# A two-layer transformer trunk on one core: the last Down units by accumulator, ScalarE's order fixed at gate/up, smaller and later loads

## The chip, the cores and the metric

The kernel runs on one core of one Trainium2 chip, in one launch. A core has five engines that run their own instruction streams side by side: TensorE (PE, the matmuls; PEld are its weight loads), VectorE (DVE), ScalarE (ACT), GpSimd (POOL) and SyncE (SP, which here only issues DMAs). An engine takes its instructions strictly in the order of its program; an instruction that waits for another engine holds up all that stand behind it. The metric is device time in microseconds (us): the median of several runs of the whole kernel.

## The reference, cut to what matters

The kernel computes two layers of an encoder trunk over one sequence of 1024 tokens with 1024 features, all in fp32. `mod` is a matrix product of a condition vector with large weights (adaLN). There are two layers, the hidden width F is 2816, and `ya`, `yb`, `yc` are three attentions over parts of `proj`; `yc` normalises its q and k, times `gq_ax` and `gk_ax`, and turns them by rotary tables.

```python
cond = jax.nn.silu(c)
for l in range(DEPTH):
    mod = cond @ w_mod[l] + b_mod[l]
    sh_a, sc_a, gt_a, sh_f, sc_f, gt_f = [m[:, None, :] for m in split_cols(mod, (D,) * 6)]
    h = rms_norm(x, g_attn[l]) * (1 + sc_a) + sh_a
    proj = h @ w_in[l]
...
    y = jnp.concatenate([rms_norm(ya, ga), rms_norm(yb, gb), rms_norm(yc, gc)], axis=-1)
    x = x + gt_a * (y @ w_o[l])

    h = rms_norm(x, g_ffn[l]) * (1 + sc_f) + sh_f
    gate, up = split_cols(h @ w_gu[l], (F, F))
    x = x + gt_f * ((jax.nn.silu(gate) * up) @ w_down[l])
return rms_norm(x, g_final)
```

## The kernel before

**Arithmetic.** An fp32 product is made of three TensorE matmuls: each operand is split into a high part (`...h`, `hi`, a rounded CAST on ScalarE) and the remainder (`...l`, `lo`, a subtraction on VectorE or GpSimd), and high x high, low x high and high x low are added in a PSUM bank (`mm3`). The feed-forward products go by a Strassen-like scheme with 7 products of quarter size in place of 8; the operands of some products are sums of blocks. `PRODUCTS` lists the seven of a quad of gate/up with the operand of the activations and one of three PSUM banks: `(1,"11",a) (2,"21",b) (6,"t2",a) (5,"t1",c) (7,"t3",a) (3,"22",c) (4,"t4",a)`. Products on the same bank follow each other, and each stands on the sum already in it; before product 7 adds onto bank a, ScalarE must have copied product 6 out of it (`COPY sg<-ps_w`), and so on.

**Stages of a layer.** Norm and input projections (`ps_c`, `ps_ab`, `ps_v`); attention (the middle of the layer); output projection (`ps_o`); gate/up (`ps_w`); Down (`ps_d`). Gate/up has 22 quads q, of 7 products with 12 matmuls each. Of the first 7 quads (`EARLY`) products 1 and 2 are made first, since their activations (`ht`... from blocks `11`, `21`) are ready soonest; after them come products 6, 5, 7, 3, 4 of quads 0 to 6, then quads 7 to 21 whole. The operands `t3`, `22` and `t4` of the activations (`ht3h/ht3l`, `h22h/h22l`, `ht4h/ht4l`) are made from the blocks `xb` of x by `t3_part` and `t4_part`, row block by row block, between these two loops. They overwrite `xb`, whose memory (tags x0 to x3) is then used for the raw weights of odd quads: `wr` (a DMA of 512 KB into x2 and one into x3) and their sums `ws`. A class `Ahead` makes the parts of the weights (`wpt`, hi by ScalarE, lo by VectorE or GpSimd) up to 8 products ahead of their use: `ahead.get()` first fills to 8, then hands out one.

Down has 7 products in the order 1, 2, 6, 7, 4, 5, 3, of 11 units each, 77 units u in all. A unit has four banks (`acc_a` or `acc_b`, one for each 128 output features) with 3 matmuls each, 12 in all; at the end of most products `residual` adds a bank to the block `xb` of x. Beside the units a generator `beside` takes a step for each: the squares of the finished half of x, its 1/rms (`rstd`), and in the last layer the turned, scaled output of that half (`out_turn`: four PE transposes into `ps_f`; `out_scale`: times 1/rms and g_final, `gf`, then a DMA out). In layer 0 it is the norm of the next layer instead.

Beside gate/up of layer 0, from quad 7 on, `mod_stream` makes adaLN products that are needed later on VectorE (`acc`), splits them (`acch`, `accl`), and `mod_flush` sums them over partitions by two matmuls a piece (`ps_mod`). Each `yield` hands control back to the loop of products.

**What sets the order.** All instructions are issued through a helper, `issue` in the class `Engine`, so that every row of the profile has its line, L49, and one goes by the names of tiles. A scheduler orders the instructions of each engine by its own estimates, unless the engine is pinned: `pin([act], True)` makes each further ScalarE instruction depend on the one issued before it, so that ScalarE has them in the order in which the code issues them. Before, SP is pinned in gate/up and Down, and ScalarE and VectorE in some places, not where gate/up begins.

Of the kernel before, what the change touches and what calls it, by code (L numbers as in the profile page):

```python
# [19 lines left out]
P = 128  # L20
D = 1024
S = 1024
KC = D // P
H = 512
FF = 2816
NF = FF // P
NB = NF // 2
# [53 lines left out]
def bc(ap, shape):  # L81
    return ap.to_broadcast(shape)
# [3 lines left out]
def trunk(ctx: ExitStack, tc, A, C, out):  # L86
# [5 lines left out]
    def pin(engines, on):  # L92
        for e in engines:
            e.pinned = on
# [260 lines left out]
    def mod_stream(psp, shared, until):  # L355


        pl, tag, bufs, width = shared
        acc = None
        while todo and todo[0] < until:  # L360
            l, g = todo[0]
            first = going["step"]
            if first == 0:
                going["acc"] = cp.tile([P, 1024], F32, name="acc", tag="acc")
            acc = going["acc"]
            halves = [(k, c0) for k in range(first, KC) for c0 in range(0, 1024, width)]
            loads = {}

            def load(i):
                k, c0 = halves[i]  # L370
                st = loads[i] = pl.tile([P, width], F32, name="wmt", tag=tag, bufs=bufs)
                g0 = g * 1024 + c0
                sp.dma_start(st, A["w_mod"][l, k * P : (k + 1) * P, g0 : g0 + width])

            if halves:
                load(0)
                yield
            for i, (k, c0) in enumerate(halves):
                if i + 1 < len(halves):
                    load(i + 1)  # L380
                mod_add(k, acc[:, c0 : c0 + width], loads.pop(i))
                yield
            going["step"] = KC
            mod_parts(slice(0, width), shared)
            while going["step"]:
                yield
                yield
                mod_flush(psp)
            yield

# [145 lines left out]
    cc_cm, ccp = open_pool("cc", side="right")  # L536
# [4 lines left out]
    csts = []  # L541
# [4 lines left out]

    def gains_load(pl, l):
        g8 = pl.tile([P, 8, 64], F32, name="g8")
        sp.dma_start(g8[:, 0:6, :], bc(A["gq_ax"][l][None, None, :], [P, 6, 64]))
        sp.dma_start(g8[:, 6:8, :], bc(A["gk_ax"][l][None, None, :], [P, 2, 64]))  # L550
        pool.tensor_scalar(
            out=g8[:, 0:6, :], in0=g8[:, 0:6, :], scalar1=0.125, scalar2=None, op0=ALU.mult
        )
        for _ in range(4):
            rope_load(pl)
        return g8
# [260 lines left out]
    for l in range(2):  # L817
# [1100 lines left out]
        for q in range(EARLY):  # L1918
            for i in range(2):
                a = [w[:, 4 * i : 4 * i + 4] for w in early[q]]  # L1920
                gu_product(q, PRODUCTS[i], a)
            if q + 4 < EARLY:
                early.append(first_cols((q + 4) % 2 * FF + (q + 4) // 2 * 2 * P))
            elif raw0 is None:
                raw0 = gu_raw(0)
            if q == 0:
                next(norm)
            if q == 1:
                rows = next(norm)
            if 1 <= q < 5:  # L1930
                bs.append(t2_part(q - 1, rows))
            if q == 1:
                t3_part(0, *bs[0])
                t4_part(0, *bs[0])
            if q == EARLY - 2:
                ahead.fill(5)
        for part in (t3_part, t4_part):
            for q in range(1, 4):
                part(q, *bs[q])
        pin([sp], True)  # L1940
        for q in range(NF):
            if q % 2 == 0:
                gu_start(q // 2)
            if q < EARLY:
                up = q % 2
                e = sg[q // 2][0][:, 0:H]
                if up:
                    pool.tensor_tensor(out=e, in0=e, in1=quads[q]["11"], op=ALU.mult)
            for i, p in enumerate(PRODUCTS[2 if q < EARLY else 0 :]):
                gu_product(q, p, ahead.get())  # L1950
                if i == 1 and q < EARLY and not up:
                    act.activation(e, quads[q]["11"], AF.Silu)
                ahead.fill()
                g_step()
                if q >= EARLY:
                    next(mods_due, None)
# [7 lines left out]
        def out_turn(half, j, nh):  # L1964

            t0 = half * H + j * P
            ps = psl.tile([P, 4, P], F32, name="ps_f", tag="mm")
            for i in range(4):
                pe.transpose(ps[:, i, :], xt[:, nh * 4 + i, t0 : t0 + P], ident)
            return half, j, nh, ps.rearrange("p a b -> p (a b)")  # L1970
# [122 lines left out]
        def square_add(ssq, n, half):  # L2093
            sq = square(n, half, "sq", 2)
            dve.tensor_tensor(out=ssq, in0=ssq, in1=sq, op=ALU.add)
# [20 lines left out]
        def odd_squares():  # L2116
            odd.append(square(1, 1, "ssqo", 1))
            yield
            for n in (3, 5, 7):
                square_add(odd[0], n, 1)  # L2120
                yield

        beside = iter(())
        for u in range(NU):
            i, t = divmod(u, NB)
            num, _, bank = DOWN[i]
            for what in due.get(u, ()):
                what()
            ahead.fill(4)
            if u % 2 == 0 and (u + 6) // 2 <= (NU - 1) // 2:  # L2130
                b_load((u + 6) // 2)
            for _ in range(3 if steps else 0):
                g_step()
            if u == 5:
                xt = blocks(xp)
            if t == 0 and num == 2:
                acc_b = [psl.tile([P, 512], F32, name="ps_d", tag="mm") for _ in range(4)]
            banks = acc_a if bank == "a" else acc_b
            a, b = ahead.have.pop(0)
            for j in range(4):  # L2140
                js = slice(j * P, (j + 1) * P)
                mm3(
                    banks[j], a[:, 0, js], a[:, 1, js], b[:, 0], b[:, 1],
                    num in (1, 2, 5) and t == 0, t == NB - 1, skip_group_check=True,
                )
            next(beside, None)
            if u >= NU - 2 and not last_layer:
                if u == NU - 2:
                    wC = []
                wC.append(split_w(w_in_src(1, C_COLS, len(wC)), 2, eng=dve))  # L2150
            if t < NB - 1:
                continue
            m, half = {
                1: (0, 0), 2: (0, 0), 6: (0, 1), 7: (1, 1), 4: (1, 0), 5: (1, 1), 3: (0, 1),
            }[num]
            for j in range(4):
                residual(banks[j], 2 * j + m, slice(half * H, half * H + H), 40)
            if num == 4:
                close(w2_cm)
                close(w1_cm)  # L2160
                if last_layer:
                    fn_cm, fnp = open_pool("fin", side="right")
                    gf = fnp.tile([P, D], F32, name="gf")
                    sp.dma_start(gf, bc(A["g_final"][None, :], [P, D]))
                else:
                    h_cm, hp = open_pool("h", side="right")
                    hh = hp.tile([P, KC, S], F32R, name="hh")
                    hl = hp.tile([P, KC, S], F32R, name="hl")
                    cc_cm, ccp = open_pool("cc", side="right")
                    csts.clear()  # L2170
                    g8 = gains_load(ccp, 1)
                    spill(0)
                beside = chain(early_half(), odd_squares())
        for _ in beside:
            pass
        pin([sp], False)
        pin((act, dve), not last_layer)
        for n in range(0, KC, 2):
            square_add(odd[0], n, 1)
        if last_layer:  # L2180
            blocks_ = [(1, j, nh) for j in range(4) for nh in range(2)]
            turned = [out_turn(*b) for b in blocks_[:7]]
            r = rstd_cols(odd, D, 4, ntp, psl)
            for t in turned:
                out_scale(*t, r)
            for b in blocks_[7:]:
                out_scale(*out_turn(*b), r)
            close(fn_cm)
            close(wb_cm)
            close(nt_cm)  # L2190
            continue
# [95 lines left out]
```

## Time and profile before

| what | us |
|---|---|
| median of 3 runs | 2467.94 (2466.91 to 2469.07) |
| profiled execution | 2463.24 |
| its span | 2461.5 |
| PE busy in it | 2386.7 (97%) |
| DVE busy | 1789.8 (73%) |
| ACT busy | 1204.2 (49%) |
| POOL busy | 754.3 (31%) |

The profiled execution is 4.70 us shorter than the median of the runs. A timeline row has the start in us from the start of the span, the duration, the engine, the line, the operation, the tile written, the tiles read, the shape and the count of merged instructions; `[0.42 <-ACT sg L49]` means that the engine sat idle for 0.42 us before the row, until ScalarE's work on `sg` released it. A matmul's duration is modelled: matmuls overlap, and the distance between starts, not the duration, tells what one costs. `PEclk` is the granted TensorE clock of a stretch, 1.00 being full speed; over the whole execution it was 0.993.

### The profile page before, as it was taken

The page shows a single profiled execution, that of the slowest core. Times are in us where ns is not written, and L with a number is a line of the kernel's source. Part 1 is how long each engine was busy: PE and PEld are TensorE (multiplying, and loading weights), DVE is VectorE, ACT ScalarE, POOL GpSimd, SP SyncE. Part 2 cuts the span into 40 slices and gives each one's busy share as a digit, 9 for nine tenths or more (in the row PEclk, how much of TensorE's full clock was granted, in tenths as well). Part 3 has the DMA queues.
Part 4 walks back from the last instruction along what each step waited for, and adds up shares of the span by engine and source line. Part 5 has one row for each costly group of instructions (what it writes and reads, how often), then busy time and mean ns, then how long its engine had stood idle before and what let it go on. Part 6 is the DMA issues. An engine that isn't in the chain of part 4 may idle for free.

```text
span 2461.5 us, 33717 instructions
## 1 busy us (share of the span) xinstructions
PE 2386.7 (97%) x11733; PEld 1962.0 (80%) x11733; DVE 1789.8 (73%) x2950; ACT 1204.2 (49%) x2290; POOL 754.3 (31%) x741
## 2 busy tenths in 40 slices
PE   8999999999999999999999999999999999999998
PEld 5777898778787787888788879987877888888886
DVE  5756899976957887586677579998687545447865
ACT  3421888954543333344443148887454333334443
POOL 1520445610344343300036124464005434430001
PEclk9999999999999999999999999999999999999999
DMA  8479016054245454596434851241534322329743
GB/s 287 138 228 291 25 27 162 26 188 137 87 142 174 154 185 145 172 268 192 140 92 123 284 164 27 58 127 55 198 94 147 127 99 95 99 100 291 209 136 107
DMA packets 305338, 356.98 MB, mean 145 GB/s; under 512 B 51964, under 2 KB 221788, under 8 KB 305168
## 3 DMA queue, kind: packets, MB, share of 16 engines
q1 hardware_dynamic: 283296, 342.07, 44.7%
q10 hardware_dynamic: 21504, 12.59, 1.9%
q8 instruction: 93, 1.52, 0.3%
q14 instruction: 77, 0.63, 0.1%
q0 software_dynamic: 368, 0.17, 0.0%
HBM read 269.79 MB, written 88.63 MB: 146 GB/s over the span
## 4 chain that ended last, share of the span: by engine, by line
PE 48%; DVE 5%; issue 4%; DMA 4%; ACT 2%; POOL 1%; SPq 0%; ACTq 0%; POOLq 0%; DVEq 0%
PE ps_w L49 20%; PE ps_d L49 14%; PE ps_o L49 4%; PE pv L49 2%; PE T L49 2%; PE ps_v L49 2%; PE sC L49 2%; DMA qkd<-qko 1%; PE ps_ab L49 1%; DMA wmt<-in_w_mod_dram 1%; DMA graw<-gpd 1%; ACT pr L49 1%; PE ps_c L49 1%; DVE acc L49 1%; DVE ws L49 1%
## 5 line engine op out<-in xcount | busy, mean ns | idle before, releaser
L49 PE MATMUL ps_d<-wpt 128*128 128x512 f32 x1848 | 426.0, 391 | 3.5 <-ACT wpt L49 3.2
L49 PEld LDWEIGHTS ps_d<-wpt 128*128 128x128 f32 x1848 | 346.6, 188 | 78.2 <-issue 3.0
L49 POOL TENSOR_SCALAR pr<-pr,rs 128x384 f32<-128x384 f32 (+2 forms) x256 | 198.7, 779 | 226.1 <-DVE rs L49 211.6
L49 POOL TENSOR_TENSOR sg<-sg,u 128x512 f32<-128x512 f32 x86 | 123.6, 1439 | 379.2 <-ACT sg L49 126.9
L49 PE MATMUL pv<-pt,vs 128*128 128x256 f32 x1088 | 181.4, 296 | 13.3 <-DVE y L49 7.8
L49 ACT CAST wpt<-w 128x512 fp32r<-128x512 f32 x154 | 95.5, 620 | 194.2 <-PE ps_d L49 175.3
L49 DVE TENSOR_TENSOR pt<-T,pt 128x512 fp32r<-128x512 f32 x272 | 178.2, 680 | 4.2 <-ACT pt L49 2.4
L49 PE MATMUL T<-identr,pr 128*128 128x128 f32 x1208 | 177.4, 274 | 3.3 <-POOL pr L49 1.3
L49 ACT COPY u<-ps_w 128x512 f32<-128x512 f32 x128 | 75.1, 587 | 201.4 <-PE ps_w L49 201.4
L49 DVE TENSOR_TENSOR wpt<-w,wpt 128x512 fp32r<-128x512 f32 x154 | 108.8, 706 | 85.6 <-ACT wpt L49 83.5
L49 POOL TENSOR_TENSOR wpt<-ws,wpt 128x512 fp32r<-128x512 f32 x80 | 111.7, 1397 | 186.3 <-ACT wpt L49 137.3
L49 ACT CAST pt<-T 128x512 fp32r<-128x512 f32 x272 | 152.7, 587 | 32.1 <-PE T L49 30.0
L49 PEld LDWEIGHTS pv<-pt,vs 128*128 128x128 f32 x1088 | 144.8, 189 | 29.5 <-DVE y L49 14.3
L49 PEld LDWEIGHTS T<-identr,pr 128*128 128x128 f32 x1208 | 142.1, 141 | 22.6 <-POOL pr L49 3.6
L49 DVE SCALAR_TENSOR_TENSOR acc<-wmt,condT,acc 128x512 f32<-128x512 f32 (+1 forms) x98 | 117.2, 1207 | 50.2 <-DMA wmt<-in_w_mod_dram 49.7
L49 ACT CAST wpt<-ws 128x512 fp32r<-128x512 f32 x176 | 107.7, 622 | 64.5 <-issue 27.5
L49 DVE TENSOR_TENSOR wpt<-ws,wpt 128x512 fp32r<-128x512 f32 x96 | 86.1, 907 | 64.6 <-ACT wpt L49 64.5
L49 DVE TENSOR_REDUCE rs<-sC 128x1 f32<-128x1024 f32 x96 | 116.9, 1220 | 10.1 <-PE sC L49 10.0
L49 DVE TENSOR_TENSOR wpt<-graw,wpt 128x512 fp32r<-128x512 f32 x154 | 109.8, 713 | 18.5 <-ACT wpt L49 18.4
L49 DVE TENSOR_TENSOR ws<-wr 128x512 f32<-128x512 f32 x88 | 81.1, 924 | 50.4 <-POOL wpt L49 47.2
L49 PE MATMUL ps_w<-h22h,wpt 128*128 128x512 f32 x352 | 112.8, 402 | 4.3 <-ACT sg L49 3.6
L49 PE MATMUL sC<-qk 128*128 128x512 f32 x384 | 108.3, 404 | 6.7 <-ACT pr L49 5.1
(289 smaller groups left out, 5994.4 us busy)
## 6 DMA issues: line engine op xcount, KB each, us to landing
wr<-in_w_gu_dram SPq DMA_DIRECT2D x92, 512.0 KB, 4.1
gpd<-sg SPq DMA_DIRECT2D x154, 256.0 KB, 4.5
graw<-gpd SPq DMA_DIRECT2D x76, 512.0 KB, 3.9
w<-in_w_down_dram SPq DMA_DIRECT2D x110, 256.0 KB, 5.3
wmt<-in_w_mod_dram SPq DMA_DIRECT2D x48, 512.0 KB, 6.2
qk<-qkd SPq DMA_DIRECT2D x44, 512.0 KB, 6.7
wst<-in_w_o_dram SPq DMA_DIRECT2D x32, 512.0 KB, 4.3
wmt<-in_w_mod_dram SPq DMA_DIRECT2D x64, 256.0 KB, 3.8
```

Source lines behind the costliest of these rows:

```text
L49: ins = op(*args, **kwargs)
```

## The change

Six places change:

1. `mod_stream` hands back control four times instead of twice before each `mod_flush`, so that four products of gate/up stand between the split of a sum and its matmuls, and the stream ends later.
2. `gains_load` loads one head of `gq_ax` and one of `gk_ax` (64 values for each of 128 partitions) instead of 6 and 2 heads; GpSimd scales one head and copies it to the others.
3. The load of the next layer's `gains_load` moves from the end of Down's product 4 (unit 54) to unit 60.
4. ScalarE is pinned from ahead of `t3_part`/`t4_part` until quad 7.
5. Down's last three units (74, 75, 76) go by accumulator: bank by bank with 9 matmuls each, and each bank's residual and square at once. The square of the fourth bank stays a tile of its own, so the sum for 1/rms reads two tiles (16 small matmuls instead of 8).
6. At the very end, four half blocks of the output are multiplied by g_final on VectorE before 1/rms is there, and multiplied by 1/rms afterwards, three on ScalarE and one on GpSimd; the other four go by one VectorE instruction each. PE, ScalarE, VectorE and GpSimd are pinned there.

```diff
@@ mod_stream
             while going["step"]:
-                yield
-                yield
+                for _ in range(4):
+                    yield
                 mod_flush(psp)
@@ gains_load
-        sp.dma_start(g8[:, 0:6, :], bc(A["gq_ax"][l][None, None, :], [P, 6, 64]))
-        sp.dma_start(g8[:, 6:8, :], bc(A["gk_ax"][l][None, None, :], [P, 2, 64]))
+        sp.dma_start(g8[:, 0, :], bc(A["gq_ax"][l][None, :], [P, 64]))
+        sp.dma_start(g8[:, 7, :], bc(A["gk_ax"][l][None, :], [P, 64]))
         pool.tensor_scalar(
-            out=g8[:, 0:6, :], in0=g8[:, 0:6, :], scalar1=0.125, scalar2=None, op0=ALU.mult
+            out=g8[:, 0, :], in0=g8[:, 0, :], scalar1=0.125, scalar2=None, op0=ALU.mult
         )
+        pool.tensor_copy(g8[:, 1:6, :], bc(g8[:, 0:1, :], [P, 5, 64]))
+        pool.tensor_copy(g8[:, 6, :], g8[:, 7, :])
@@ gate/up
+        pin([act], True)
         for part in (t3_part, t4_part):
             for q in range(1, 4):
                 part(q, *bs[q])
         pin([sp], True)
         for q in range(NF):
+            if q == EARLY:
+                pin([act], False)
@@ Down
+        LAST = 3
...
+            if u == 60 and not last_layer:
+                csts.clear()
+                g8 = gains_load(ccp, 1)
...
-            a, b = ahead.have.pop(0)
-            for j in range(4):
+            take = 1 if u < NU - LAST else LAST if u == NU - LAST else 0
+            ab_ = [ahead.have.pop(0) for _ in range(take)]
+            for j in range(4 if take else 0):
                 js = slice(j * P, (j + 1) * P)
-                mm3(
-                    banks[j], a[:, 0, js], a[:, 1, js], b[:, 0], b[:, 1],
-                    num in (1, 2, 5) and t == 0, t == NB - 1, skip_group_check=True,
-                )
+                for k, (a, b) in enumerate(ab_):
+                    mm3(
+                        banks[j], a[:, 0, js], a[:, 1, js], b[:, 0], b[:, 1],
+                        num in (1, 2, 5) and t == 0, t + k == NB - 1, skip_group_check=True,
+                    )
+                if take == LAST:
+                    residual(banks[j], 2 * j, slice(H, S), 40)
+                    if j < 3:
+                        square_add(odd[0], 2 * j, 1)
+                    else:
+                        odd.append(square(2 * j, 1, "sq", 2))
...
@@ end of the last layer
-            blocks_ = [(1, j, nh) for j in range(4) for nh in range(2)]
-            turned = [out_turn(*b) for b in blocks_[:7]]
+            pin((pe, act, dve, pool), True)
+            turned = [out_turn(1, j, 0)[3] for j in range(4)]
+            os = [fnp.tile([P, H], F32, name="o", tag="o", bufs=10) for _ in range(4)]
+            for o, ps in zip(os, turned):
+                dve.tensor_tensor(out=o, in0=ps, in1=gf[:, 0:H], op=ALU.mult)
             r = rstd_cols(odd, D, 4, ntp, psl)
-            for t in turned:
-                out_scale(*t, r)
+            for j in range(4):
+                r0 = H + j * P
+                ps = out_turn(1, j, 1)[3]
+                o, rj = os[j], r[:, j : j + 1]
+                if j < 3:
+                    act.activation(o, o, AF.Copy, scale=rj)
+                else:
+                    pool.tensor_scalar(
+                        out=o, in0=o, scalar1=rj, scalar2=1.0, op0=ALU.mult, op1=ALU.mult
+                    )
+                sp.dma_start(out[0, r0 : r0 + P, 0:H], o)
+                o = fnp.tile([P, H], F32, name="o", tag="o", bufs=10)
+                dve.scalar_tensor_tensor(
+                    out=o, in0=ps, scalar=rj, in1=gf[:, H:D], op0=ALU.mult, op1=ALU.mult
+                )
...
```

ScalarE where gate/up of layer 0 goes from products 6 and 5 of quad 0 to product 7 (`ps_w_6262` before and `ps_w_6264` after is bank a of quad 0; `wpt_6604`, `_6607`, `_6611` before, and `wpt_6606`, `_6609`, `_6613` after, are quad 1's weights, made from sums `ws`). Before:

```order
L49 CAST ht3h_6226<-xb_5737 128x512
L49 CAST ht3h_6226<-xb_5739 128x512
L49 CAST ht3h_6226<-xb_5741 128x512
L49 COPY sg_6590<-ps_w_6262 128x512
L49 ACT_TABLE_LOAD
L49 ACTIVATE sg_6590<-u_6275 128x512
L49 CAST ht4h_6222<-xb_5738 128x512
L49 ACTIVATE sg_6808<-u_6377 128x512
L49 CAST ht4h_6222<-xb_5740 128x512
L49 COPY u_6661<-ps_w_6262 128x512
L49 COPY sg_6591<-ps_w_6631 128x512
L49 CAST ht4h_6222<-xb_5742 128x512
```

The same place after:

```order
L49 CAST ht3h_6228<-xb_5743 128x512
L49 ACTIVATE h22h_6226<-xb_5740,mod0_82 128x512
L49 CAST ht4h_6224<-xb_5740 128x512
L49 ACTIVATE h22h_6226<-xb_5742,mod0_82 128x512
L49 CAST ht4h_6224<-xb_5742 128x512
L49 ACTIVATE h22h_6226<-xb_5744,mod0_82 128x512
L49 CAST ht4h_6224<-xb_5744 128x512
L49 CAST wpt_6606<-ws_6602 128x512
L49 CAST wpt_6609<-ws_6602 128x512
L49 CAST wpt_6613<-ws_6603 128x512
L49 COPY sg_6592<-ps_w_6264 128x512
L49 CAST wpt_6630<-ws_6603 128x512
```

The copy of bank a stood directly behind the three casts of `ht3h`; it now stands behind six instructions for `h22h` and `ht4h` and three casts of quad 1's weights.

TensorE at the same place, after (`ps_w_6308` is quad 1's bank a; `ht3h` on `ps_w_6264` is product 7 of quad 0):

```order
L49 MATMUL ps_w_6633<-ht1h_6222,wpt_6526 128x512 x2
L49 MATMUL ps_w_6633<-ht1l_6223,wpt_6526 128x512
L49 MATMUL ps_w_6308<-ht2h_6220,wpt_6606 128x512 x2
L49 MATMUL ps_w_6308<-ht2l_6221,wpt_6606 128x512
L49 MATMUL ps_w_6264<-ht3h_6228,wpt_6530 128x512 x2
L49 MATMUL ps_w_6264<-ht3l_6229,wpt_6530 128x512
```

Three matmuls of quad 1 now stand ahead of product 7 of quad 0, where before product 7 came directly behind product 5 (`ht1`).

SP in Down of layer 0, before (`graw` are the hidden values that Down reads, `g` the q/k scales, `cst` the rotary tables, `xd` the spilled x):

```order
L49 DMA graw<-gpd 128x1024 x6
L49 DMA g_10939<-in_gq_ax_dram 128x6x64
L49 DMA g_10939<-in_gk_ax_dram 128x2x64
L49 DMA cst<-const_rope_dram 128x128 x4
L49 DMA xd<-xb 128x512 x8
L49 DMA graw<-gpd 128x1024 x2
L49 DMA cst<-const_rope_dram 128x128
L49 DMA graw<-gpd 128x1024 x3
```

And after:

```order
L49 DMA graw<-gpd 128x1024 x6
L49 DMA xd<-xb 128x512 x8
L49 DMA graw<-gpd 128x1024 x3
L49 DMA g_11065<-in_gq_ax_dram 128x64
L49 DMA g_11065<-in_gk_ax_dram 128x64
L49 DMA cst<-const_rope_dram 128x128 x5
L49 DMA graw<-gpd 128x1024 x2
```

The scales and tables stood ahead of the eight spills and the next `graw`; they now stand behind them and three `graw`.

VectorE at the very end, before:

```order
L49 SCALAR_TENSOR_TENSOR xb<-ps_d,mod_83,xb 128x512 x4
L49 TENSOR_TENSOR sq<-sq 128x512 x4
L49 RECIPROCAL rstd<-rstd 128x4
L49 SCALAR_TENSOR_TENSOR o<-ps_f,rstd,gf 128x512 x5
```

And after, from the last residual but one:

```order
L49 SCALAR_TENSOR_TENSOR xb<-ps_d,mod_83,xb 128x512
L49 TENSOR_TENSOR sq<-sq 128x512
L49 SCALAR_TENSOR_TENSOR xb<-ps_d,mod_83,xb 128x512
L49 TENSOR_TENSOR o<-ps_f,gf 128x512 x2
L49 TENSOR_TENSOR sq<-sq 128x512
L49 TENSOR_TENSOR o<-ps_f,gf 128x512 x2
L49 TENSOR_TENSOR sq<-sq 128x512
L49 RECIPROCAL rstd<-rstd 128x4
L49 SCALAR_TENSOR_TENSOR o<-ps_f,rstd,gf 128x512 x4
```

Of the four additions of squares two remain behind the last residual, and four multiplications by `gf` have come in between.

More of the change, by code (lines that the diff above doesn't have):

```diff
@@ L2150, in trunk @@
                 wC.append(split_w(w_in_src(1, C_COLS, len(wC)), 2, eng=dve))
-            if t < NB - 1:
+            if t < NB - 1 or num == 3:
                 continue
             m, half = {
-                1: (0, 0), 2: (0, 0), 6: (0, 1), 7: (1, 1), 4: (1, 0), 5: (1, 1), 3: (0, 1),
+                1: (0, 0), 2: (0, 0), 6: (0, 1), 7: (1, 1), 4: (1, 0), 5: (1, 1),
             }[num]
@@ L2169, in trunk @@
                     cc_cm, ccp = open_pool("cc", side="right")
-                    csts.clear()
-                    g8 = gains_load(ccp, 1)
                     spill(0)
@@ L2177, in trunk @@
         pin((act, dve), not last_layer)
-        for n in range(0, KC, 2):
-            square_add(odd[0], n, 1)
         if last_layer:
-            blocks_ = [(1, j, nh) for j in range(4) for nh in range(2)]
-            turned = [out_turn(*b) for b in blocks_[:7]]
-            r = rstd_cols(odd, D, 4, ntp, psl)
-            for t in turned:
-                out_scale(*t, r)
-            for b in blocks_[7:]:
-                out_scale(*out_turn(*b), r)
+            pin((pe, act, dve, pool), True)
[3 more added lines that the diff above has]
+                dve.tensor_tensor(out=o, in0=ps, in1=gf[:, 0:H], op=ALU.mult)
+            r = rstd_cols(odd, D, 4, ntp, psl)
+            for j in range(4):
[13 more added lines that the diff above has]
+                )
+                sp.dma_start(out[0, r0 : r0 + P, H:D], o)
+            pin((pe, act, dve, pool), False)
             close(fn_cm)
```

## The prediction, made before the changed kernel was run

> **What bounds the kernel now.** I read the page first, then the waits of TensorE, then the timelines of the places that the diff touches.
>
> ```profile
> span 2461.5 us, 33717 instructions
> PE 2386.7 (97%) x11733; PEld 1962.0 (80%) x11733; DVE 1789.8 (73%) x2950; ACT 1204.2 (49%) x2290; POOL 754.3 (31%) x741
> PE ps_w L49 <- ACT sg L49: 4.4, 4, 1.8
> PE ps_w L49 <- ACT u L49: 3.8, 5, 1.2
> PE ps_d L49 <- ACT wpt L49: 3.2, 2, 2.5
> ```
>
> PE is busy for 97% of the span, so only what leaves PE without work, or slows its clock, moves the end. The change removes no matmul. What it can win is in the waits: all of gate/up's for ScalarE's copies are 8.2 us, Down's for weights 3.2. What it can lose is a wait put into one of these places. First, gate/up's begin in layer 0:
>
> ```profile
> 637.18 1.88 DVE L49 TENSOR_TENSOR ht3l<-xb,ht3h 128x512 fp32r<-128x512 f32 x3
> 637.88 19.49 SPq L49 DMA_DIRECT2D wr<-in_w_gu_dram  x7
> 638.37 0.40 PE L49 MATMUL ps_w<-ht1l,wpt 128*128 128x512 f32 x1
> 638.55 0.59 ACT L49 COPY sg<-ps_w 128x512 f32<-128x512 f32 x1 [0.64 <-DVE ht3l L49]
> 638.98 0.74 DVE L49 SCALAR_TENSOR_TENSOR h22l<-xb,mod,h22h 128x512 fp32r<-128x512 f32 x1
> 639.19 0.73 PE L49 MATMUL ps_w<-ht3h,wpt 128*128 128x512 f32 x2 [0.42 <-ACT sg L49]
> 639.64 0.74 DVE L49 SCALAR_TENSOR_TENSOR xb<-xb,mod,t 128x512 f32<-128x512 f32 x1
> 643.16 0.73 PE L49 MATMUL ps_w<-ht4h,wpt 128*128 128x512 f32 x2 [0.93 <-ACT u L49]
> 646.39 1.22 PE L49 MATMUL ps_w<-h22h,wpt 128*128 128x512 f32 x2 [1.79 <-ACT sg L49]
> 649.31 0.69 DVE L49 TENSOR_TENSOR ws<-ws,wr 128x512 f32<-128x512 f32 x1
> 650.03 1.66 ACT L49 CAST wpt<-ws 128x512 fp32r<-128x512 f32 x3 [1.25 <-DVE ws L49]
> 650.67 0.39 PE L49 MATMUL ps_w<-ht4l,wpt 128*128 128x512 f32 x1
> 648.00:649.00 1.00, 1.00 (x4) 0.81 (x3) 1.00 (x2) 0.63 (x1) 0.12 (x1) 0.50 1.10 349
> 650.00:651.00 1.00, 1.00 (x6) 0.82 (x5) 0.13 (x2) 0.97 (x2) 0.00 (x0) 1.00 0.00 0
> 1840.63 0.73 PE L49 MATMUL ps_w<-ht3h,wpt 128*128 128x512 f32 x2 [0.39 <-ACT sg L49]
> 1847.83 1.22 PE L49 MATMUL ps_w<-h22h,wpt 128*128 128x512 f32 x2 [1.79 <-ACT sg L49]
> ```
>
> The last two are layer 1's, the same to 0.03 us. The rows of stretches give, after the length, busy time and count of PE, PEld, DVE, ACT, POOL, then PE's clock, DMA share, GB/s. PE idles 0.42 + 0.93 + 1.79 = 3.14 us, then runs at half clock until 650. From the end of 638.37 (638.77) to 650.67 are 11.90 us with 29 matmuls; at the 0.23 us of one (30.18 us for 132, below) they need 6.7, so 11.90 - 3.14 - 6.7 = 2.1 us go to the slow clock.
>
> **1. ScalarE in fixed order.** The order moves the copy of quad 0's bank a (638.55 above), for which PE's product 7 waits, behind three casts of quad 1's weights. These need the sums `ws`, the sums need both raw weight loads, and the second load goes into the memory of a block that `ht4l` of the first row block still reads:
>
> ```profile
> SPq L49 <- DVE ht4l L49: 5.1, 1, 5.1
> DMA to landing us min/median/max: 3.4/4.1/6.6
> ```
>
> SP waited 5.1 us for it, and a raw load lands 4.1 us after its issue (all of them: 3.4 to 6.6). The chain after the change: VectorE is done with `ht3l` at 637.18 + 1.88 = 639.06; now one `h22l` and three `xb` stand ahead of the first `ht4l`, 4 x 0.66 (638.98 to 639.64) = 2.6, and the `ht4l` itself 0.63 (1.88/3): 642.3. Second load landed at 646.4. Two sums of 0.7 (650.03 less 649.31): 647.8. Three casts at 1.66/3: 649.5. The copy, 0.59: 650.1. PE had been without work since 638.77 but for three matmuls of quad 1 that were moved ahead (0.7): 650.1 - 638.77 - 0.7 = 10.6 us without work in place of 3.14, so +7.5. The slow clock behind it I leave at 2.1: a stall comes before it in both cases. `h22h` and `ht4h`, done meanwhile, cost PE no more. So +7.5 a layer, **+15.0** in both. Bounds for a layer: landing at 3.4 and 1 us of the slow clock gone, +5.8; landing at 6.6, +10.0.
>
> [...]
>
> **2. The q/k scales.** In Down of layer 0:
>
> ```profile
> 1189.10 1.38 SPq L49 DMA_DIRECT2D g<-in_gq_ax_dram  x1
> 1193.07 12.38 SPq L49 DMA_DIRECT2D xd<-xb  x8
> 1196.00:1198.00 2.00, 2.00 (x11) 1.65 (x10) 1.90 (x4) 1.48 (x4) 0.00 (x0) 1.00 0.11 29
> 1202.00:1206.00 4.00, 4.00 (x19) 3.34 (x18) 0.00 (x0) 0.00 (x0) 1.18 (x1) 1.00 0.96 355
> 1210.31 0.62 ACT L49 CAST wpt<-graw 128x512 fp32r<-128x512 f32 x1 [9.33 <-DMA graw<-gpd]
> 1210.98 7.63 PE L49 MATMUL ps_d<-wpt 128*128 128x512 f32 x24 [2.50 <-ACT wpt L49]
> 1226.18 30.18 PE L49 MATMUL ps_d<-wpt 128*128 128x512 f32 x132 [0.71 <-ACT wpt L49]
> ```
>
> While the scales' small pieces move, from 1189 to about 1201, the queue carries 29 GB/s; the spills `xd` behind them flow only from 1202 on at 355, and the `graw` behind those arrives 2.5 us too late. After the change the spills go at once, the `graw` behind them, and the scales (a quarter of the bytes) come last, for use in the next layer. The 2.50 and 0.71 go, and the slow clock: 7.63 less 24 x 0.23 = 2.0. **-5.2**. Bounds -5.2 and -2.0 (the scales now delay the two `graw` behind them by what remains of a quarter of 12 us). GpSimd's two copies stand beside nothing that waits: 0. At the kernel's start the same load is far from its use: 0.
>
> **3. Four products ahead of each `ps_mod`.**
>
> ```profile
> 798.96 0.49 PE L49 MATMUL ps_mod<-acch,onesr 128*128 128x512 f32 x1 [0.86 <-DVE acch L49]
> 801.24 0.50 PE L49 MATMUL ps_mod<-accl,onesr 128*128 128x512 f32 x1 [1.79 <-DVE accl L49]
> 926.67 0.50 PE L49 MATMUL ps_mod<-accl,onesr 128*128 128x512 f32 x1 [0.39 <-DVE accl L49]
> ```
>
> PE's only waits for these splits. With two products (5.5 us) more in between, VectorE has been through them: 0.86 + 1.79 + 0.39 = **-3.0**. The stream gets longer and ends by the end of gate/up, 104 of 105 hand-overs by my count, so nothing is flushed in a row there. Bounds: -4.2, with one wait of 1.2 for `u` gone that follows on the same VectorE load; +1.0, if the later sums collide in their turn (one of 0.86).
>
> **4. Down's last three units, and the end.**
>
> ```profile
> 2443.94 2.79 DVE L49 SCALAR_TENSOR_TENSOR xb<-ps_d,mod,xb 128x512 f32<-128x512 f32 x4 [6.90 <-PE ps_d L49]
> 2446.65 3.07 DVE L49 TENSOR_TENSOR sq<-sq 128x512 f32<-128x512 f32 x4
> 2449.77 1.05 PE L49 MATMUL ps_st<-onesr,sq 128*128 128x1 f32 x8 [0.69 <-DVE sq L49]
> 2451.44 3.38 DVE L49 SCALAR_TENSOR_TENSOR o<-ps_f,rstd,gf 128x512 f32<-128x512 f32 x5
> 2455.00:2456.00 1.00, 0.00 (x0) 0.00 (x0) 0.00 (x0) 0.00 (x0) 0.85 (x1) 0.50 1.05 385
> 2458.00:2459.00 1.00, 0.00 (x0) 0.00 (x0) 0.00 (x0) 0.00 (x0) 0.00 (x0) 0.50 1.02 379
> ```
>
> The last residual of a bank still ends at about 2446.7, since PE ends with the same matmul. Behind it stood four additions (3.07). Now stand there two additions, since the generator steps for units 74 and 75 come after the whole block of three, and four multiplications by `gf`: at 0.68 (3.38/5) and 0.77 (3.07/4) some 4.3, of which half a microsecond overlaps: +0.7 for 1/rms. Its sum now has 16 small matmuls for 8 in 1.05: +0.85. Behind 1/rms compute is shorter, yet the end was set by the queue, which carries the 8 outputs of 256 KB at 380 GB/s until 2459. They start later by 1.55 less what the shorter, unbroken start gives back (about 0.45): **+1.1**. Bounds -0.7 (1/rms not later, the start shorter) and +2.2. In layer 0 the same 8 further small matmuls: **+0.9**, bounds 0 and 1.0.
>
> **The sum.** 15.0 - 5.2 - 3.0 + 1.1 + 0.9 = +8.8. On the profiled execution's 2463.24 that is 2472.0; this execution lies 4.70 below the median of the runs, 2467.94, and on that the forecast is 2476.7.
>
> **Rivals.**
> (a) The other side: the fixed order does only what its words say, and the casts of quad 1 find their sums done. Then the first stage's 3.14 + 2.1 go in both layers: -10.5 - 5.2 - 3.0 + 2.0 = -16.7, 2451.2. It decides at the copy: it would have to run by 638.8, so the second raw load landed some 10 us sooner than `ht4l` lets it go. Against it: the 5.1 us that SP waits. For it: the estimate of a memory's release rests on one wait. Chance 0.07.
> (b) Within 0.2% (4.9 us; about what a measurement of this kernel can tell from no change): the stall at its lower bound, 2 x 5.8, and the rest as above: +5.4, or +4.2 with the wait for `u` gone too: 2472.1. Chance 0.17.
> (c) The fixed order goes on until quad 7, and copies of quads 1 to 6 come behind casts in the same way: at 1.2 us (the longest wait for `u`) in six quads of two layers +14, so 2491. For it: every cast is now ahead of the next copy by rule. Against it: a bank's copy has a whole product, 12 x 0.23 = 2.8 us, until it is needed, and copy and cast need 1.2. Chance 0.10.
> (d) The end doesn't do what it says: the two squares that still wait behind the multiplications show it. It is in the sum.
>
> The forecast itself has 0.66. Low end: stall +5.8 twice, scales -5.2, mods -4.2, end -0.7, layer 0 none: +1.5, or 2469; with rival (a) beyond it I set 2467. High end: 2 x 10.0 would give 2487 with the rest as above, and part of (c) lies there: 2487. Slower by over 0.2% (above 2472.9): 0.66 + 0.10 = 0.76; same 0.17; faster 0.07.
>
> **What would show it.** Right: PE waits for ScalarE's `sg` for about 10 us near 650 and again 1201 us later, with `wpt` casts just ahead of that copy, themselves waiting for VectorE's `ws`, and that for a `wr` load; no wait for `wpt` near 1211; none for `acch`; 1/rms at about 2 us behind its old distance from the last residual. Wrong: the copy `sg` within a microsecond of the end of product 5, which would take 15 us out of the sum; new waits for `u` in quads 1 to 6; or PE waiting for `graw` behind the scales' new place.

## The result: slower by 0.6%

| kernel | median us | runs |
|---|---|---|
| before | 2468.51 | 2466.91 to 2471.68, 4 runs |
| changed | 2481.91 | 2478.61 to 2483.84, 4 runs |

The ratio is 1.006, with a 95% interval from 1.0044 to 1.0075: 10.9 to 18.5 us. The profiled execution of the changed kernel took 2483.84 us (span 2482.1), 20.6 us more than the profiled one of before. The times are thus 13.4 us apart by the medians and 20.6 by the two profiles; the rest of this section says where the 20.6 lie, and how much of them the change has nothing to do with.

First gate/up's begin in layer 0, from the timeline of the changed kernel (start, duration, engine; in brackets the idle time ahead and its releaser):

```profile
641.61 0.40 PE L49 MATMUL ps_w<-ht1l,wpt 128*128 128x512 f32 x1
642.85 2.07 DVE L49 SCALAR_TENSOR_TENSOR xb<-xb,mod,t 128x512 f32<-128x512 f32 x3
644.84 0.68 DVE L49 TENSOR_TENSOR ht4l<-xb,ht4h 128x512 fp32r<-128x512 f32 x1
649.21 0.69 DVE L49 TENSOR_TENSOR ws<-wr 128x512 f32<-128x512 f32 x1 [0.56 <-DMA wr<-in_w_gu_dram]
650.72 1.66 ACT L49 CAST wpt<-ws 128x512 fp32r<-128x512 f32 x3 [4.21 <-DVE ws L49]
651.39 1.52 PE L49 MATMUL ps_w<-ht2h,wpt 128*128 128x512 f32 x2 [9.38 <-ACT wpt L49]
652.28 0.57 ACT L49 COPY sg<-ps_w 128x512 f32<-128x512 f32 x1
653.13 1.06 PE L49 MATMUL ps_w<-ht3h,wpt 128*128 128x512 f32 x2
1859.38 1.52 PE L49 MATMUL ps_w<-ht2h,wpt 128*128 128x512 f32 x2 [9.32 <-ACT wpt L49]
```

Product 5 of quad 0 ends at 642.0. TensorE then has nothing until 651.39, when the first of three casts of quad 1's weights is done; the copy of bank a comes behind the casts at 652.28, and product 7 at 653.13. The casts waited 4.21 us for the sums, the sums for the raw load, and that load for the first `ht4l`, done at 645.52 (3.9 us after product 5's last start, 641.61). Layer 1 does the same (9.32 us). Before, TensorE's waits at this place were 0.42, 0.93 and 1.79 us.

In the waits of TensorE the first row is new; the row of `sg`, four waits with 4.4 us together before, is now one wait of 4.3 us at another place:

```profile
PE ps_w L49 <- ACT wpt L49: 18.7, 2, 9.4
PE ps_w L49 <- ACT sg L49: 4.3, 1, 4.3
PE ps_st L49 <- DVE sq L49: 3.0, 1, 3.0
PE ps_d L49 <- ACT wpt L49: 0.7, 1, 0.7
```

The wait for `acch` is gone, those for `accl` fall from 2.6 to 0.2 us, and the 2.5 us for a weight in Down of layer 0 are gone as well (0.7 is what stays of 3.2). The 4.3 us are the longer mod stream, beside quad 20 of layer 0, at its end:

```profile
1006.14 7.28 SPq L49 DMA_DIRECT2D gpd<-sg  x3
1013.47 0.43 SPq L49 DMA_DIRECT2D wmt<-in_w_mod_dram  x1
1016.19 0.69 DVE L49 TENSOR_TENSOR sg<-sg 128x512 f32<-128x512 f32 x1 [0.98 <-DMA gpd<-sg]
1016.80 0.75 DVE L49 SCALAR_TENSOR_TENSOR acc<-wmt,condT,acc 128x512 f32<-128x512 f32 x1
1018.19 0.68 DVE L49 TENSOR_TENSOR u<-u,ps_w 128x512 f32<-128x512 f32 x1
1018.91 0.63 ACT L49 ACTIVATE sg<-u 128x512 f32<-128x512 f32 x1 [8.05 <-DVE u L49]
1020.06 0.86 PE L49 MATMUL ps_w<-ht3h,wpt 128*128 128x512 f32 x2 [4.30 <-ACT sg L49]
```

SP sends the last `wmt` only behind three stores `gpd<-sg`. Most of the 7.28 us of that row is waiting: the third store goes at 1013.10, when VectorE has made its `sg`. In VectorE's order a subtraction `sg<-sg`, which waits 0.98 us for that store, the step `acc` and the split of its sum stand ahead of the addition `u<-u,ps_w`; ScalarE, in turn, has an `ACTIVATE` for that `u` ahead of the copy that product 7 needs. Before, the stream was over by 991 us.

The end, from Down's last bank on:

```profile
2463.80 0.74 DVE L49 SCALAR_TENSOR_TENSOR xb<-ps_d,mod,xb 128x512 f32<-128x512 f32 x1
2464.46 1.28 DVE L49 TENSOR_TENSOR o<-ps_f,gf 128x512 f32<-128x512 f32 x2
2467.63 0.68 DVE L49 TENSOR_TENSOR sq<-sq 128x512 f32<-128x512 f32 x1
2468.36 3.57 PE L49 MATMUL ps_st<-onesr,sq 128*128 128x1 f32 x16 [2.96 <-DVE sq L49]
2472.27 0.18 DVE L49 RECIPROCAL rstd<-rstd 128x4 f32<-128x4 f32 x1 [3.96 <-ACT rstd L49]
```

From the end of the last residual (2464.54) to 1/rms (2472.45) it is 7.9 us; before it was 2446.73 to 2451.34, 4.6, by this row of the kernel before:

```profile
2451.16 0.18 DVE L49 RECIPROCAL rstd<-rstd 128x4 f32<-128x4 f32 x1 [1.44 <-ACT rstd L49]
```

To see where 20.6 us arise I cut both timelines at the same matmuls. The cuts in layer 0: the last `ht1l` of quad 0 and of quad 2, the first of quad 15, the last of quad 21; Down's first and last `ps_d`. In layer 1: the last `ht1l` of quad 0 and of quad 2, and Down's last `ps_d`. Each number is the difference of two starts in the timeline of TensorE (the last one up to the span's end), in us:

| stretch | before | changed | difference |
|---|---|---|---|
| A start to quad 0, layer 0 | 638.4 | 641.6 | +3.2 |
| B quad 0 to quad 2, layer 0 | 33.4 | 40.4 | +7.0 |
| C quad 2 to 15 | 234.5 | 231.6 | -2.9 |
| D quad 15 to 21 | 123.2 | 127.9 | +4.7 |
| E Down, layer 0 | 217.0 | 212.3 | -4.7 |
| F layer 1 to quad 0 | 583.9 | 586.8 | +2.9 |
| G quad 0 to quad 2, layer 1 | 33.4 | 40.5 | +7.1 |
| H quad 2 to Down's last matmul | 572.3 | 573.1 | +0.8 |
| I the end | 15.9 | 18.8 | +2.9 |

The short piece from quad 21 to Down is 0.3 less. A and F hold attention and projections, where the change does little: the first scales' load at the kernel's start (A) and 8 further small matmuls (F). H holds the rest of layer 1. In the 13 profiled executions of this case A lies between 636.2 and 642.7 (636.2 to 642.1 in the eight with the old load) and F between 582.8 and 588.9 (582.8 to 585.9 in the nine without the further small matmuls). So of A and F only what a trace shows as a longer instruction is counted as the change's, the sum of the squares in layer 0; whether the other 2 us of F belong to the change isn't shown.

```profile
1274.29 1.84 PE L49 MATMUL ps_st<-onesr,sq 128*128 128x1 f32 x16
```

In the kernel before 8 matmuls take 0.95 us at 1267.35: +0.9. B + C + D + E + G + I + 0.9 is +15.0 us, which lies inside the interval of the times.

### The profile page after: what moved, and what is told of

It reads as the page before. It is cut to its first block, busy times and chain, and to the rows that moved or that the text cites. A ratio compares the mean times of both kernels' runs of the same rounds, so it can differ in the third digit from the quotient of the medians.

```text
span 2482.1 us, 33733 instructions
## 1 busy us (share of the span) xinstructions
PE 2399.1 (97%) x11749; PEld 1974.7 (80%) x11749; DVE 1778.1 (72%) x2951; ACT 1202.7 (48%) x2290; POOL 748.9 (30%) x743
## 4 chain that ended last, share of the span: by engine, by line
PE 74%; DVE 11%; DMA 6%; ACT 4%; issue 3%; POOL 2%; SPq 0%; ACTq 0%; DVEq 0%; POOLq 0%
PE ps_w L49 29%; PE ps_d L49 16%; PE ps_o L49 7%; PE pv L49 5%; PE T L49 4%; PE sC L49 3%; PE ps_v L49 3%; DMA qkd<-qko 2%; DMA wmt<-in_w_mod_dram 2%; PE ps_c L49 1%; PE ps_ab L49 1%; ACT pr L49 1%; DVE acc L49 1%; DVE ws L49 1%; PE ps_st L49 1%
## 5 line engine op out<-in xcount | busy, mean ns | idle before, releaser
L49 PE MATMUL ps_w<-ht2h,wpt 128*128 128x512 f32 x352 | 112.1, 399 | 19.2 <-ACT wpt L49 18.7
L49 DVE TENSOR_TENSOR wpt<-ws,wpt 128x512 fp32r<-128x512 f32 x96 | 78.2, 823 | 67.2 <-ACT wpt L49 67.1
L49 PE MATMUL ps_w<-ht3h,wpt 128*128 128x512 f32 x352 | 113.4, 404 | 4.8 <-ACT sg L49 4.3
```

Of the source, the lines that this page charges most:

```text
L49: ins = op(*args, **kwargs)
```

## The experiments

The theory: the fixed order costs some 7 us a layer, the mod stream is a loss of 2 to 4, Down's loads gain 4 to 5, the end loses 1.5 to 3. The rivals are told run by run. Unless a line says otherwise a run has its ratio to runs of the kernel before on the same chip (their median there 2465 to 2466 us). The stretches are those of the table.

**The pin alone, and all but the pin.** On the kernel before:

```diff
+        pin([act], True)
         for part in (t3_part, t4_part):
...
         for q in range(NF):
+            if q == EARLY:
+                pin([act], False)
```

> The kernel before with one edit of the change: ScalarE pinned from ahead of t3_part/t4_part until quad 7. Theory (the fixed order puts three casts of quad 1's weights, which wait for a raw load, ahead of the copy that product 7 of quad 0 needs): slower by 13.3 us (6.8 in layer 0 and 6.5 in layer 1, as the profile of the changed kernel has it), 2468.5 becomes about 2481.8; TensorE waits 9.4 us for wpt at gate/up's begin in each layer. Rival (the stall comes of another part of the change, such as the longer mod stream or the moved loads, and the pin alone costs nothing): within 3 us of before, and no wait over 2 us at that place.

Measured (run e1): 2481.1 us, ratio 1.0062 (1.0045 to 1.0078).

```profile
PE ps_w L49 <- ACT wpt L49: 18.9, 2, 9.5
```

B is 40.3, G 40.7. The other way about, the changed kernel without these lines:

> The changed kernel without the ScalarE pin at gate/up, all else kept. Theory: the 13.3 us of the two stalls go, 2481.9 becomes about 2468.6, no different from before; what is left of the change is then worth about nothing: scales -5.0, mod stream -4.5 + 6.6, layer 0's sum +0.9, the end +2.9, together +0.9. Rival: the pin is not what costs, and the time stays above 2478.

Measured (run e2): 2467.62 us, ratio 1.0006 (0.9993 to 1.0019), B 32.4, G 33.4. So the pin accounts for the whole loss, and all else together is worth nothing that can be measured. The rival is out in both.

**What holds the copy: the casts.** The changed kernel with its pin, but quad 0 doesn't fill up ahead:

```diff
-                gu_product(q, p, ahead.get())
+                gu_product(q, p, ahead.get() if q else ahead.have.pop(0))
...
-                ahead.fill()
+                if q or i >= 3:
+                    ahead.fill()
```

> The changed kernel, ScalarE pinned as there, but the first three products of quad 0 after the pin take their weights without filling up ahead, so that quad 1's casts are issued behind the copies of banks a and c instead of ahead of them. Theory (the casts are what holds the copy): the copy stands only behind h22h and ht4h, which end 4.5 us after product 5; TensorE's wait falls from 9.4 us to about 5.1 in each layer, and the time to about 2473 (2481.9 less 2 x 4.4). Rival (h22h and ht4h, with VectorE's work for them, hold the copy, and the casts only fill the same time): the wait stays at 9 us and the time above 2479.

Measured (run e3): 2476.03 us, ratio 1.0044 (1.0027 to 1.0061). The wait is what was forecast:

```profile
648.17 1.22 PE L49 MATMUL ps_w<-ht3h,wpt 128*128 128x512 f32 x2 [5.07 <-ACT sg L49]
```

B and G fall to 36.9 and 37.1, 3.5 us each, not 4.4. With the casts behind it, the copy still stands behind `h22h` and `ht4h`, which before it did not: so the casts are half of the loss (9.4 to 5.1 of the wait), and the six instructions of the row blocks, with the work of VectorE that they wait for, are the rest. The median came 3 us above the expectation; 1.8 of it is B and G, for the rest the spread between executions (A was 642.7, F 588.9 in the profiled one) is enough.

**The mod stream alone.** Four hand-overs on the kernel before, as in the change's first part:

> The kernel before with four hand-overs instead of two ahead of each mod_flush. Theory (from the two profiles): the waits for acch and accl go and with them 4.5 us, but the stream now runs beside quads 17 to 21 as well, where a step of it holds up the addition that a copy waits for: 6.6 us in one place near its end; net +2 us, 2470.5. Rival (the stall near the end of the stream in the changed kernel belongs to the shift of the other parts): the 4.5 us go and nothing comes, 2464.0.

Measured (run e4): 2468.82 us, ratio 1.0015 (0.9999 to 1.0031). C is 231.6 (-2.9), D 128.5 (+5.3), with the same stall, and here the step `acc` itself waits for the last `wmt`:

```profile
1004.56 0.42 SPq L49 DMA_DIRECT2D wmt<-in_w_mod_dram  x1
1007.52 0.75 DVE L49 SCALAR_TENSOR_TENSOR acc<-wmt,condT,acc 128x512 f32<-128x512 f32 x1 [0.49 <-DMA wmt<-in_w_mod_dram]
1010.78 1.22 PE L49 MATMUL ps_w<-ht3h,wpt 128*128 128x512 f32 x2 [4.17 <-ACT sg L49]
```

The stall belongs to the stream alone. Would three do?

```diff
-                yield
-                yield
+                for _ in range(3):
+                    yield
                 mod_flush(psp)
```

> The kernel before with three hand-overs ahead of each mod_flush. Theory (a split needs a little over two products on VectorE, and the new stall of the longer stream comes from its end falling beside quads 20 and 21): the 3.0 us between quads 2 and 15 go as with four, 178.8 to 175.8 us, and from quad 15 to 21 it stays near before's 123.2, since the stream ends 8 products sooner than with four: 2.5 to 3 us faster. Rival (any longer stream meets the stall): 127 us or more from quad 15 to 21.

Measured in one execution (run e10): 2469.68 us beside 2466.24. C is 232.9 (-1.6), D 125.2 (+2.0): gain and loss both lie between those of two and four hand-overs, and neither three nor four gains. The expectation that D stays is wrong, and the 127 us of its rival aren't reached either.

**The scales: pieces or place.** First one head of each and the copies, at the old place:

```diff
-        sp.dma_start(g8[:, 0:6, :], bc(A["gq_ax"][l][None, None, :], [P, 6, 64]))
-        sp.dma_start(g8[:, 6:8, :], bc(A["gk_ax"][l][None, None, :], [P, 2, 64]))
+        sp.dma_start(g8[:, 0, :], bc(A["gq_ax"][l][None, :], [P, 64]))
+        sp.dma_start(g8[:, 7, :], bc(A["gk_ax"][l][None, :], [P, 64]))
...
```

> The kernel before with one head of each scale loaded and copied by GpSimd, at the load's old place ahead of the spills. Theory (the number of small pieces is what holds up the spills and the graw behind them: 1024 pieces took some 12 us of the queue, 256 take some 3): the stretch from Down's first to its last matmul in layer 0 falls from 217.0 us to 212.3, as in the changed kernel, and TensorE's wait of 2.5 us for a weight near 1211 goes. Rival (the place ahead of the spills is what counts): it stays at 216 to 217. The gain of 4.7 us is 0.2% of the whole.

Measured in one execution (run e5): 2456.13 us; E is 212.3, the wait of 2.5 us is gone. Then the old pieces at the new place:

```diff
+            if u == 60 and not last_layer:
+                csts.clear()
+                g8 = gains_load(ccp, 1)
...
-                    csts.clear()
-                    g8 = gains_load(ccp, 1)
```

> The kernel before with the scales in their old 1024 pieces, but sent at unit 60, behind the spills and three graw. Theory of the pieces: they hold up the two graw that now stand behind them, and a wait of 0 to 2.5 us comes back some 15 us later: the stretch of Down in layer 0 at 213 to 217 us. Rival (the place alone does it): 212.3 us, as in the changed kernel.

Measured in one execution (run e6): 2464.27 us; E is 219.2, longer than before. From the waits, the timeline and two stretches of this run:

```profile
PE ps_d L49 <- DVE xb L49: 5.0, 1, 5.0
1204.86 0.43 SPq L49 DMA_DIRECT2D g<-in_gq_ax_dram  x1
1209.92 8.09 SPq L49 DMA_DIRECT2D graw<-gpd  x2
1222.42 0.62 ACT L49 CAST wpt<-graw 128x512 fp32r<-128x512 f32 x1 [4.74 <-DMA graw<-gpd]
1208.00:1212.00 4.00, 4.00 (x19) 3.34 (x18) 1.97 (x4) 2.23 (x4) 0.00 (x0) 1.00 0.08 21
1212.00:1216.00 4.00, 4.00 (x23) 3.40 (x23) 1.49 (x4) 2.58 (x4) 0.00 (x0) 1.00 0.13 37
```

The 1024 pieces hold up what stands behind them: here the first of the two `graw`, while the DMAs carry 21 and 37 GB/s. TensorE's wait of 5.0 us is put down to `xb`, a residual that frees its bank; this residual stands in VectorE's order behind a weight made from that `graw`. The place gains nothing; the pieces do. E with the old pieces at the old place is 214.5 to 218.4 in seven executions (mean 216.4), with the new ones 212.3 to 213.0 in five: 4 us.

**The end.** The last three units by accumulator and the new end, on the kernel before (the change's parts 5 and 6):

> The kernel before with the last three units by accumulator and the new end, nothing else. Theory (1/rms comes later by two additions of squares behind four multiplications, and by a sum of 16 small matmuls that take 2.1 us at full clock or 3.6 at half, for 8 in 1.05): from Down's last bank in layer 1 to the end of the span 17.3 to 18.8 us for 15.95, and in layer 0 0.9 more: slower by 2 to 4 us, 2468 to 2470 beside 2466. Rival (the end only looks longer since its start moved, and by accumulator the residuals are done sooner): no change, or faster by up to 1 us.

Measured (run e7): 2467.22 us, ratio 1.0007 (0.9993 to 1.0021); I is 18.2. The time can't tell 2 us; the profile can. The two parts weren't run apart. Next the same with the leftover squares first and with one sum:

```diff
+            if u == NU - LAST:
+                for _ in beside:
+                    pass
             take = 1 if u < NU - LAST else LAST if u == NU - LAST else 0
...
-                    if j < 3:
-                        square_add(odd[0], 2 * j, 1)
-                    else:
-                        odd.append(square(2 * j, 1, "sq", 2))
+                    square_add(odd[0], 2 * j, 1)
```

> As the kernel before with the new end, but with the squares of blocks 1, 3, 5, 7 all taken ahead of the last three units, and the fourth bank's square added to the same sum, so that the sum has 8 small matmuls again. Theory: one addition behind the last residual in place of two behind four multiplications, and 8 small matmuls: the end takes 15.0 to 16.0 us, no longer than before's 15.95, and the time is that of before within 1 us. Rival (the multiplications by gf ahead of 1/rms are what costs): still over 17 us.

Measured (run e8): 2464.29 us, ratio 0.9997 (0.9983 to 1.0011); I is 14.3, 1.6 us less than before.

```profile
2447.28 0.68 DVE L49 TENSOR_TENSOR sq<-sq 128x512 f32<-128x512 f32 x1
2448.02 1.05 PE L49 MATMUL ps_st<-onesr,sq 128*128 128x1 f32 x8 [0.98 <-DVE sq L49]
2449.41 0.18 DVE L49 RECIPROCAL rstd<-rstd 128x4 f32<-128x4 f32 x1 [0.24 <-ACT rstd L49]
```

From the last residual's end (2445.43 + 0.75) to 1/rms (2449.59) it is 3.4 us, against 7.9 in the changed kernel: two multiplications and one addition stand ahead of the sum, not four and two, and the sum is short. Its expectation had it no better than before; it is.

**Another order of row blocks.** In the kernel before, the copy of bank c writes where `ht4l` of row block 2 reads. So that block first:

```diff
-        for part in (t3_part, t4_part):
-            for q in range(1, 4):
+        for part, qs in ((t3_part, (1, 2, 3)), (t4_part, (2, 1, 3))):
+            for q in qs:
                 part(q, *bs[q])
```

> The kernel before with the t4 and 22 parts of the row blocks made in the order 2, 1, 3 in place of 1, 2, 3, nothing pinned. Theory (in the kernel before the copy of bank c waits because it writes into the memory of a block that ht4l of row block 2 still reads, and that bank's product then waits 1.79 us): with row block 2 first the copy comes some 3 us sooner, TensorE's 0.93 and 1.79 us go or shrink below 1 us together, the clock stays up, and gate/up's begin (from product 5 of quad 0 to quad 2) falls from 33.4 or 32.4 us to about 30 in each layer. Rival (VectorE's whole work for h22l and ht4l sets the pace, whatever its order): it stays above 32.

Measured in one execution (run e9): 2463.55 us beside 2466.24; B 33.9, G 35.4. B and G go the rival's way: the wait of 0.93 us is gone, but product 3 waits 1.89 us, about as before, since the `ht4l` that was to come sooner took 1.77 us, beside GpSimd's multiplication of `sg` (in the changed kernel, where GpSimd has nothing to do at that time, 0.68). And quad 1's weights, whose load is now released later, put a new wait behind it:

```profile
639.47 1.77 DVE L49 TENSOR_TENSOR ht4l<-xb,ht4h 128x512 fp32r<-128x512 f32 x1
641.97 0.96 PE L49 MATMUL ps_w<-h22h,wpt 128*128 128x512 f32 x2 [1.89 <-ACT sg L49]
650.50 0.51 PE L49 MATMUL ps_w<-ht2h,wpt 128*128 128x512 f32 x1 [1.14 <-ACT wpt L49]
```

**What gains, together.** The small pieces at their old place with the mended end, no pin, two hand-overs:

> The kernel before with the two pieces that gained by themselves: the scales in 256 pieces with GpSimd's copies, at their old place, and the new end with its squares taken first and one sum (as in the run e8). No pin at gate/up, two hand-overs. Theory (gains of separate places add): 4.7 us in Down of layer 0 and 1.6 us at the end, no loss elsewhere: 0.25% faster than before, ratio about 0.9975, 2460 beside 2466. Rival (what is gained in Down of layer 0 is taken back in the stages behind it, whose waits on transfers end at a time of their own): ratio 0.9995 or more.

Measured (run e11): 2462.88 us against 2465.68, ratio 0.9989 (0.9979 to 1.0000). E is 213.0 and I 14.3, as the parts had them; the ratio lies between the theory's 0.9975 and the rival's 0.9995, and at its upper end it is no gain. It is the fastest by ratio of all that were timed in several runs.

## Why the prediction was right, and where its sum was off

It said slower, 2476.7 in a range of 2467 to 2487; 2481.9 was measured. Its change of +8.8 us lies below the interval of 10.9 to 18.5, and some 6 us below the +15.0 of the stretches. That the result lies well inside the range is luck: the high end is added up wrongly. Stalls of 10.0 in place of 7.5, twice, add 5.0 to 2476.7, which is 2481.7 and not 2487, and only the part of rival (c) laid on top is left as a reason for more; the measured time lies 0.2 us past 2481.7. Its steps:

1. **ScalarE in fixed order: +15.0.** Right in mechanism, and in size to 1 us. The chain came as worked out: `ht4l` at 3.9 us past product 5's last start (predicted 642.3, 3.9 past 638.4), the load, the sums, three casts, the copy. B and G give +14.1. Nearly all of it is time without work (9.38 us and a new wait of 0.67 in layer 0, against 3.14: 6.9 of B's 7.0), so the slow clock behind it (0.50 from 651 to 655 us, before 0.50 to 0.52 from 646 to 649) cost about the same as before, as the prediction left it. One detail differs: the wait stands in the row of `wpt`, since three matmuls of quad 1 had been put ahead of product 7. The runs e1 and e2 show that the pin alone does it; e3 shows that the casts are half.
2. **The scales: -5.2.** Right: -4.7 between the two profiles, some -4 over the executions. The wait of 0.71 us, which was to go, is still there; what went is the 2.50 us and the slow clock behind them (0.66 and 0.50 in the two stretches of 2 us from 1212 to 1216 before). The 29 GB/s that it put on the whole of 1189 to 1201 is the lowest stretch of 2 us: 134 and 135 come before 1193, 29 to 85 from 1194 to 1202. What it laid on place and pieces together is the pieces' (e5, e6); its lower bound, that the later scales delay the two `graw` behind them, is what happens with the old pieces.
3. **Four products ahead of each `ps_mod`: -3.0.** This step failed. The -3.0 came (C, -2.9), but the stream's new length put a loss of 4.7 to 5.3 us beside quads 15 to 21 (D): +1.7 to +2.4 in all. The prediction had the stream's end right and bounded the whole step at +1.0, by one wait of 0.86 seen before; it did not ask what stands on SP and VectorE where the stream had not been. That is 4.7 of the 6 us by which the sum is short.
4. **The end: +1.1.** Sign right, size low: +2.9 in the changed kernel, +1.3 to +2.9 over the executions with this end. The multiplications and squares came as written (the sum starts 3.8 us behind the last residual, 3.0 before); the 16 small matmuls were costed as 0.85 more than 1.05 us, and took 2.06 us in the run without the pin, where the clock stood at 1.00, and 3.57 in the changed kernel, where it stood at 0.50. **Layer 0's sum: +0.9** was right (1.84 against 0.95).

Rival (a), the copies on time: its decisive point, the copy by 638.8, was not met. Rival (b), the stall at its lower bound of 5.8 a layer: B and G give 7.0 and 7.1. Rival (c), further waits for `u` in quads 1 to 6: there is one of 0.67 us in each layer, at 675.87 and 1884.02, which the runs without the pin don't have; that is 1.3 of the 14 us. Rival (d) stood in the sum and is shown by e7 and e8.

## What to carry to other kernels

An order fixed as the code issues it is only as good as that order: ahead of a pin, read for each engine what stands between an instruction that another engine waits for and the last one before it, and follow each of those to the transfer that it needs. When side work is spread over a longer time, the place where it now ends has to be read too, on the queues as well. Here a broadcast load of 1024 small pieces held up the transfers behind it at both places tried (at the old one the DMAs carried 29 to 85 GB/s from 1194 to 1202 us, at the later one 21 and 37 from 1208 to 1216; E was 216.4 us in the mean and 219.2); 256 pieces helped (212.3 to 213.0), a later place did not.

## What the runs showed of the hardware that I had not expected

**The clock after the same gaps.** In two executions with equal waits at gate/up's begin (0.42, 0.93, 1.79 and 0.42, 0.93, 1.78 us within 8 us), the granted clock was 0.51 for the two us around the end of the third in the kernel before (first row) and stayed at 1.00 with four hand-overs (the other two), whose edit comes later in the program:

```profile
646.00:648.00 2.00, 1.61 (x4) 1.33 (x5) 1.92 (x3) 0.95 (x2) 1.59 (x1) 0.51 1.09 375
648.48 0.73 PE L49 MATMUL ps_w<-h22h,wpt 128*128 128x512 f32 x2 [1.78 <-ACT sg L49]
648.00:650.00 2.00, 1.52 (x7) 1.25 (x8) 1.91 (x3) 1.05 (x2) 1.50 (x1) 1.00 1.09 373
```

B is 33.4 in the one and 32.4 in the other: 1 us of 2468 hangs on it, and another in layer 1. At the end it is more: behind the same 2.96 us without work, the 16 small matmuls took 3.57 us in the changed kernel, at a clock of 0.50, and 2.06 us in the run without the pin, at 1.00:

```profile
2452.23 2.06 PE L49 MATMUL ps_st<-onesr,sq 128*128 128x1 f32 x16 [2.96 <-DVE sq L49]
2452.40:2453.40 1.00, 1.00 (x11) 1.00 (x11) 0.00 (x0) 0.00 (x0) 0.00 (x0) 1.00 0.06 16
```

In the first pair no single gap is longer than 1.79 us: in the kernel before the clock stood at 0.51 at the end of gaps of 3.14 us together, and with four hand-overs it stayed at 1.00 with gaps of 3.13. In the second pair it stood at 0.50 and at 1.00 behind 2.96 us. Why the clock falls in one execution and not in the other isn't shown. At the end, 16 small transposes stand directly ahead of the 2.96 us (1.91 us in the changed kernel), and no run shows whether the gap alone would do.

**The spread of one execution.** The stretch from the start to gate/up of layer 0 took 636.2 to 642.7 us in 13 profiled executions, that of layer 1 582.8 to 588.9, with nearly the same work in them. Two profiles alone would have put 6 us of that on the change. The spread goes with the granted clock: over the first stretch it was 0.99 in four of the five shortest executions (636.2 to 639.3) and 0.98 in the other one (638.7) and in all from 640.3 on; over the second it was 0.99 in those of 584.8, 585.1, 586.8 and 588.9 us and 1.00 in the others (582.8 to 585.9). Why the clock differs between executions isn't shown. Whether the smaller first load at the kernel's start costs 1 or 2 us there (five executions with it 639.1 to 642.7, eight without it 636.2 to 642.1) stays open.
